# Routing keys of the chosen pairs by comparison of positions with row offsets, instead of one-hots over 50 candidates

## The chip, the cores and the metric

The kernel runs on one core of a Trainium2 chip. The metric is the device time of one execution in microseconds (us). Before the change the median of three runs is 2036.78 us (2036.38 to 2038.27).

## The reference, cut to what matters

The model has two layers. Each is a mixer (five small head groups behind one input projection, then an output projection) followed by PEER, a feed-forward part that picks 16 of 16,384 experts for each of 8 heads and each of 256 tokens. The change lies in the picking:

```python
q  = (xn @ wq).reshape(b, s, 8, 2, 128)
sc = einsum('bshjc,hjkc->bshjk', q, subkeys)         # two score rows of 128 keys per head
top_s, top_i = top_k(sc, 16)                         # 16 best keys of each row
cand = top_s[..., 0, :, None] + top_s[..., 1, None, :]   # 16 x 16 sums
best, ci = top_k(cand, 16)                           # 16 best pairs
i1 = take_along_axis(top_i[..., 0, :], ci // 16)     # first key of each chosen pair
i2 = take_along_axis(top_i[..., 1, :], ci % 16)      # second key
g  = softmax(best)
act = gelu(u_tab[i1*128 + i2] . xn) * g              # then  sum of act * v_tab[i1*128 + i2]
```

Since both rows are sorted, a pair (a, b) can be among the 16 best only if (a+1)(b+1) <= 16. That leaves 50 of 256 sums. The kernel keeps these 50 in 16 rows: row a has `PAIR_LEN[a]` = 16 // (a+1) sums and begins at position `PAIR_OFF[a]`. The chosen positions are numbers from 0 to 49.

## The kernel before

Nothing is gathered. All experts' products are computed densely: 128 blocks of `u_t` and 128 blocks of `v_t` per layer, each a 128x1024 f32 weight tile, are streamed from HBM. The class `Stream` loads a block (`w_raw`, three buffers), rounds it to `w_hi` on ScalarE (line 82) and takes the rest `w_lo = w_raw - w_hi` on VectorE (line 84; 10 of the 612 on GpSimd). `w_hi` and `w_lo` have three buffers each, so a `w_hi` may be written only when TensorE has finished with the block three places earlier. `out_t_job` then does 24 matmuls per block, at lines 235 to 237: `w_hi` with `xh`, `w_hi` with `xl`, `w_lo` with `xh`. `pair_job` runs two blocks and hands the sums to ScalarE (line 930 for `u_t`).

In a PEER phase the blocks are 16 of `wq`, 128 of `u_t`, 128 of `v_t`. The routing runs as background work beside `wq` and the first `u_t` blocks: generators whose steps are emitted between the half pairs (`Background.advance`, with a cost noted at each `yield`). `score_steps(tt)` (lines 787 to 822), for each of two tiles of 128 tokens, has the key scores from TensorE (line 799) and takes the 16 best with five VectorE instructions per row (805 to 809); GpSimd makes the 50 sums `cand` and, in the same way, the 50 sums of keys `ecand` = 128 i1 + i2 (818, 821). `best_steps(tt)` takes the 16 best sums of each head (832 to 836), and then for each head builds a 50x16 one-hot of the chosen positions (846), multiplies it with `ecand` (848) and sums over the 50 (853). Lines 856 to 859 split the result into i1 and i2; three transposes on TensorE and three ScalarE copies (869 to 871) give `i1T`, `i2T`, `gT`.

When both tiles are routed, `gate_step` spreads the gates: 32 groups of 8 tokens per layer, one after each `u_t` pair. `gate_one_hots` builds `a2` (888) and eight `ag` (893) on VectorE, `gate_group` multiplies them on TensorE (903) and applies them (907, 908). The `u_t` results of the first 64 blocks lie in the first half of one large tile `H`; the routing's tables are carved from its second half, so they read as `H` in every row.

The order on each engine is fixed when the program is built: a scheduler simulates the engines and places instructions by readiness and priority, `w_hi` and `w_lo` 300 places ahead. On the chip each engine works its queue in that order.

Of the kernel before, what the change touches and what calls it, by code (L numbers as in the profile page):

```python
# [136 lines left out]
def build(tc, x, mem, w_in, w_kv, w_out, wq, u_t, v_t, subk, pool_w, conv_pw, vec, dist, inv_count, ind, out, depth=2,  # L137
          dbg=None):
    nc = tc.nc
    V, A, G = nc.vector, nc.scalar, nc.gpsimd  # L140
# [14 lines left out]
    with (  # L155
# [17 lines left out]

        ind_t = cp.tile([P, 3, P], F32, name="ind_t")
        ones_m, ind64, ind32 = ind_t[:, 0, :], ind_t[:, 1, :], ind_t[:, 2, :]
        iota_i = cp.tile([P, NPAIR, 16], BF16, name="iota_i")
        G.iota(iota_i, pattern=[[1, NPAIR], [0, 16]], base=0, channel_multiplier=0, allow_small_or_imprecise_dtypes=True)
        iota_f = cp.tile([P, NK], F32, name="iota_f")
        G.iota(iota_f, pattern=[[1, NK]], base=0, channel_multiplier=0, allow_small_or_imprecise_dtypes=True)
        mhalf = cp.tile([P, 1], F32, name="mhalf")  # L180
# [553 lines left out]
        def peer_phase(l, pp, pb):  # L734
            nonlocal vecs

            def psum(shape, name):
                return pb.tile(shape, F32, name=name, tag="misc")

            def acc_tile(i, shape, name):  # L740
                return (pb if i % 2 else accp).tile(shape, F32, name=name, tag="acc")
# [10 lines left out]
            def carve(n, dt=F32):  # L752
                nonlocal o
                s = hf[:, o:o + n]
                o += n
                assert o <= NK * T
                return s if dt is F32 else s.bitcast(dt)

            qT = carve(4096)
            xs = qT[:, 0:2 * D].rearrange("p (a d) -> p a d", a=2)  # L760
            qT = qT.rearrange("p (h j t) -> p h j t", h=8, j=2)
            rms_transposed(pp, psum, xt, xs, vv("norm_ffn"), xh, xl, True)
            sk = carve(2048).rearrange("p (a k) -> p a k", a=16)
            nc.sync.dma_start(sk, subk[l])
# [3 lines left out]
            gT = pt([P, T], "gT")  # L768

            work = [carve(128) for _ in range(2)]  # L770
            oh = [carve(8 * NPAIR, BF16).rearrange("p (n k) -> p n k", k=16) for _ in range(2)]
            pr = [carve(16 * NPAIR).rearrange("p (k n) -> p k n", k=16) for _ in range(2)]
            tabs = []
            for tt in range(2):
                tabs.append(dict(
                    top_s=carve(256).rearrange("p (h j k) -> p h j k", h=8, j=2),
                    top_i=carve(256, U32).rearrange("p (h j k) -> p h j k", h=8, j=2),
                    top_f=carve(256).rearrange("p (h j k) -> p h j k", h=8, j=2),
                    cand=carve(8 * NPAIR).rearrange("p (h n) -> p h n", h=8),
                    ecand=carve(8 * NPAIR).rearrange("p (h n) -> p h n", h=8),  # L780
                    best=carve(P).rearrange("p (h k) -> p h k", h=8),
                    bi=carve(P, U32).rearrange("p (h k) -> p h k", h=8),
                    bib=carve(P // 2, BF16).rearrange("p (h k) -> p h k", h=8),
                    es=carve(P).rearrange("p (h k) -> p h k", h=8),
                    ei=carve(3 * P, I32).rearrange("p (a k) -> p a k", a=3),
                    fin=carve(3 * P).rearrange("p (a k) -> p a k", a=3),
                    gs=carve(8)))
            done = {"q": 0, "routing": False, "u": 0, "g": 0}

            def score_steps(tt):  # L790

                tb = tabs[tt]
                for hq in range(4):
                    while done["q"] < 2 * hq + 2:
                        yield None
                    ps = acc_tile(hq, [P, 4, NK], "ps_sc")
                    for r in range(4):
                        hj = 4 * hq + r
                        nc.tensor.matmul(ps[:, r, :], qT[:, hj // 2, hj % 2, tt * P:(tt + 1) * P], sk[:, hj, :],  # L799
                                         start=True, stop=True)  # L800
# [10 lines left out]
                top_s, top_f = tb["top_s"], tb["top_f"]  # L811
                V.tensor_copy(top_f, tb["top_i"])
                V.tensor_scalar(top_f[:, :, 0, :], top_f[:, :, 0, :], 128.0, None, op0=ALU.mult)
                for dst, src in ((tb["cand"], top_s), (tb["ecand"], top_f)):
                    for a in range(9):
                        n, off = PAIR_LEN[a], PAIR_OFF[a]
                        if a < 8:
                            G.tensor_add(dst[:, :, off:off + n], src[:, :, 1, 0:n],
                                         src[:, :, 0, a:a + 1].to_broadcast([P, 8, n]))
                        else:  # L820
                            G.tensor_add(dst[:, :, off:off + 8], src[:, :, 0, 8:16],
                                         src[:, :, 1, 0:1].to_broadcast([P, 8, 8]))
                yield 0.6

            def best_steps(tt):

                tb = tabs[tt]
                best, bi, cand, ecand = tb["best"], tb["bi"], tb["cand"], tb["ecand"]
                wk = work[tt][:, :NPAIR]
                for h in range(8):  # L830
                    m0, m1 = best[:, h, 0:8], best[:, h, 8:16]
                    V.max(m0, cand[:, h, :])
                    V.max_index(bi[:, h, 0:8], m0, cand[:, h, :])
                    V.match_replace(wk, m0, cand[:, h, :], -3e38)
                    V.max(m1, wk)
                    V.max_index(bi[:, h, 8:16], m1, wk)
                    yield 0.8
                fin, gs = tb["fin"], tb["gs"]
# [3 lines left out]
                V.tensor_copy(tb["bib"], bi)  # L842
                yield 0.6

                def one_hot(h):
                    V.tensor_tensor(out=oh[h % 2], in0=iota_i, in1=tb["bib"][:, h, None, :].to_broadcast([P, NPAIR, 16]),
                                    op=ALU.is_equal)
                    V.tensor_mul(pr[h % 2], oh[h % 2].rearrange("p n k -> p k n"),  # L848
                                 ecand[:, h, None, :].to_broadcast([P, 16, NPAIR]))

                for h in range(8):
                    one_hot(h)
                    V.tensor_reduce(tb["es"][:, h, :], pr[h % 2], axis=AX.X, op=ALU.add)  # L853
                    yield 2.4
                ei = tb["ei"]
                V.tensor_copy(ei[:, 0, :], tb["es"].rearrange("p h k -> p (h k)"))
                V.tensor_scalar(ei[:, 1, :], ei[:, 0, :], 7, None, op0=ALU.arith_shift_right)
                V.tensor_scalar(ei[:, 2, :], ei[:, 0, :], 127, None, op0=ALU.bitwise_and)
                V.tensor_copy(fin[:, 0:2, :], ei[:, 1:3, :])
                yield 1.0  # L860
# [212 lines left out]
```

## Time and profile before

| | us |
|---|---|
| median of three runs | 2036.78 |
| the profiled execution, its own time | 2035.27 |
| its span | 2033.5 |
| TensorE busy | 1973.2 (97%) |
| VectorE busy | 1494.1 (73%) |
| ScalarE busy | 985.4 (48%) |
| GpSimd busy | 165.0 (8%) |

PE is TensorE's matmul side, PEld its weight load, DVE VectorE, ACT ScalarE, POOL GpSimd, SP the engine that issues the DMAs. A line is that of the kernel before. The first layer's PEER phase runs from 173.6 us to about 1020 us; its `u_t` part ends at 669 us. The second layer repeats it some 1006 us later.

### The profile page before, as it was taken

The numbers are of one execution on the slowest core, as the hardware profiler recorded it, in microseconds if no ns is written. First come the engines' busy times: TensorE is split into PE (matmuls) and PEld (weight loads), VectorE is DVE, ScalarE is ACT, GpSimd is POOL, SyncE is SP. The second block draws the span as 40 slices with busy tenths as digits, with TensorE's granted clock in tenths as the row PEclk, the third lists the DMA queues.
The fourth block names the chain that finished last, engine by engine and source line by source line (L and its number), as shares of the span: only waits on it lengthen the run. The fifth ranks groups of instructions, "written<-read, shape, count | busy, mean of one in ns | idle before, by whom it ended". The sixth has DMA issues, their size and how long they took to land.

```text
span 2033.5 us, 33742 instructions
## 1 busy us (share of the span) xinstructions
PE 1973.2 (97%) x13122; PEld 1811.5 (89%) x13122; DVE 1494.1 (73%) x2809; ACT 985.4 (48%) x1474; POOL 165.0 (8%) x201
## 2 busy tenths in 40 slices
PE   8889999999999999999999999999999999999999
PEld 7878999899999888888898789999999998888887
DVE  6975899878898655555578669997789975555555
ACT  6664445344444544444466644444444344444443
POOL 3720101000000000000036201010000000000000
PEclk9999999999999999999999999999999999999999
DMA  5325445444444555555543254445434445555554
GB/s 212 115 74 175 167 150 172 162 153 143 144 137 156 199 195 189 194 189 194 189 169 111 86 169 166 162 151 172 149 136 146 140 152 194 188 193 190 194 189 156
DMA packets 92768, 331.50 MB, mean 163 GB/s; under 512 B 10816, under 2 KB 11712, under 8 KB 92352
## 3 DMA queue, kind: packets, MB, share of 16 engines
q1 hardware_dynamic: 92608, 329.34, 46.7%
q8 instruction: 103, 1.69, 0.3%
q14 instruction: 57, 0.47, 0.1%
HBM read 328.25 MB, written 1.05 MB: 162 GB/s over the span
## 4 chain that ended last, share of the span: by engine, by line
PE 82%; DVE 10%; ACT 3%; issue 3%; POOL 3%; DMA 1%; SPq 0%; DVEq 0%; POOLq 0%; ACTq 0%
PE ps_mm L237 13%; PE ps_mm L235 13%; PE ps_mm L236 13%; PE acc_v L265 11%; PE acc_v L268 11%; PE acc_v L264 11%; PE ps_g L903 5%; DVE w_lo L84 3%; DVE H L848 2%; POOL cv_ac L433 1%; ACT w_hi L82 1%; DVE ag L893 1%; DVE H L853 1%; PE ps_sc L799 1%; PE acc_o L264 1%
## 5 line engine op out<-in xcount | busy, mean ns | idle before, releaser
L84 DVE TENSOR_TENSOR w_lo<-w_raw,w_hi 128x1024 fp32r<-128x1024 f32 x602 | 743.0, 1235 | 394.6 <-ACT w_hi L82 392.6
L82 ACT CAST w_hi<-w_raw 128x1024 fp32r<-128x1024 f32 x612 | 641.5, 1049 | 786.7 <-PE ps_mm L236 443.0
L237 PE MATMUL ps_mm<-xh,w_lo 128*128 128x256 f32 x2624 | 748.3, 286 | 16.8 <-DVE w_lo L84 16.5
L235 PE MATMUL ps_mm<-xh,w_hi 128*128 128x256 f32 x2624 | 752.2, 288 | 2.6 <-ACT H L930 2.3
L236 PE MATMUL ps_mm<-xl,w_hi 128*128 128x256 f32 x2624 | 746.2, 285 | 0.1
L237 PEld LDWEIGHTS ps_mm<-xh,w_lo 128*128 128x128 f32 x2624 | 504.7, 192 | 22.9 <-DVE w_lo L84 21.9
L235 PEld LDWEIGHTS ps_mm<-xh,w_hi 128*128 128x128 f32 x2624 | 504.0, 192 | 4.7 <-ACT H L930 3.3
L236 PEld LDWEIGHTS ps_mm<-xl,w_hi 128*128 128x128 f32 x2624 | 505.4, 193 | 1.0 <-DVE xl L226 0.6
L265 PE MATMUL acc_v<-w_lo,a_hi 128*128 128x512 f32 x1016 | 316.5, 392 | 0.0
L268 PE MATMUL acc_v<-w_hi,a_lo 128*128 128x512 f32 x1016 | 315.4, 392 | 0.0
L264 PE MATMUL acc_v<-w_hi,a_hi 128*128 128x512 f32 x1016 | 274.1, 391 | 0.0
L268 PEld LDWEIGHTS acc_v<-w_hi,a_lo 128*128 128x128 f32 x1016 | 191.0, 188 | 42.3
L264 PEld LDWEIGHTS acc_v<-w_hi,a_hi 128*128 128x128 f32 x1016 | 190.9, 188 | 41.7
L265 PEld LDWEIGHTS acc_v<-w_lo,a_hi 128*128 128x128 f32 x1016 | 191.0, 188 | 40.6
L941 ACT CAST a_hi<-H 128x512 fp32r<-128x512 f32 x128 | 79.3, 621 | 154.1 <-PE acc_v L265 150.2
L943 DVE TENSOR_TENSOR a_lo<-H,a_hi 128x512 fp32r<-128x512 f32 x128 | 88.5, 693 | 77.5 <-ACT a_hi L941 77.5
L893 DVE TENSOR_SCALAR ag<-iota_f,i1T,gT 128x128 f32<-128x128 f32 x512 | 142.0, 343 | 0.0
L903 PE MATMUL ps_g<-ag,a 128*128 128x128 f32 x1024 | 125.8, 275 | 1.1 <-DVE ag L893 1.1
L903 PEld LDWEIGHTS ps_g<-ag,a 128*128 128x128 f32 x1024 | 120.6, 192 | 1.5 <-DVE ag L893 1.5
L888 DVE TENSOR_TENSOR a<-iota_f,i2T 128x1024 f32<-128x1024 f32 x64 | 77.8, 1218 | 0.0
L908 DVE TENSOR_TENSOR H<-ps_g,H 128x240 f32<-128x240 f32 (+31 forms) x128 | 66.2, 523 | 0.1
L195 POOL MEMSET mm_kz<- 128x1024 f32 x2 | 1.9, 951 | 698.1 <-DMA w_raw<-w_kv 698.1
(242 smaller groups left out, 1464.2 us busy)
## 6 DMA issues: line engine op xcount, KB each, us to landing
w_raw<-u_t SPq DMA_DIRECT2D x256, 512.0 KB, 3.3
w_raw<-v_t SPq DMA_DIRECT2D x256, 512.0 KB, 3.2
w_raw<-w_in SPq DMA_DIRECT2D x40, 512.0 KB, 3.3
w_raw<-wq SPq DMA_DIRECT2D x32, 512.0 KB, 3.4
w_raw<-w_out SPq DMA_DIRECT2D x20, 512.0 KB, 3.2
w_raw<-w_kv SPq DMA_DIRECT2D x8, 512.0 KB, 3.4
H<-subk SPq DMA_DIRECT2D x2, 1024.0 KB, 4.8
mem_t<-mem SPq DMA_DIRECT2D x4, 256.0 KB, 6.3
```

Of the source, the lines that this page charges most:

```text
L82: self.nc.scalar.copy(hi, r)
L84: (self.nc.gpsimd if on_pool else self.nc.vector).tensor_sub(lo, r, hi.bitcast(F32))
L235: nc.tensor.matmul(ps, wh, xh[:, c, :], start=(c == 0), stop=False)
L236: nc.tensor.matmul(ps, wh, xl[:, c, :], start=False, stop=False)
L237: nc.tensor.matmul(ps, wl, xh[:, c, :], start=False, stop=(c == NC - 1))
L264: nc.tensor.matmul(accs[tt][hf], ah[:, s], hi[:, n], start=start, stop=False)
L265: nc.tensor.matmul(accs[tt][hf], ah[:, s], lo[:, n], start=False, stop=False)
L268: nc.tensor.matmul(accs[tt][hf], al[:, s], hi[:, n], start=False, stop=False)
L893: V.tensor_scalar(ag[:, t, :], iota_f, i1T[:, k:k + 1], gT[:, k:k + 1], op0=ALU.is_equal, op1=ALU.mult)
L903: nc.tensor.matmul(ps[:, t, :], a2[:, 4 * q + t, :], ag[:, 4 * q + t, :], start=True, stop=True)
L941: A.copy(ah, src)
L943: V.tensor_sub(al, src, ah.bitcast(F32))
```

## The change

The first key of a chosen pair at position n is the sum, over the 16 rows a, of [n >= `PAIR_OFF[a]`] times (key of row a minus key of row a-1). The same comparisons with the row lengths give the start of n's row; n minus that start is the place b in the row, and the second key is the sum over k of [b >= k] times (key k minus key k-1). All heads of a tile are done in one instruction each, on 128x(8x16x16) bf16 operands, with the sum over 16 as four halvings (1024, 512, 256, 128 elements). The key differences `diff` are made at the end of `score_steps` (817 to 821 in the new file) and ScalarE spreads them to `dx` (854). `ecand` and its GpSimd sums go, as do the conversions at 856 to 859. The large bf16 tiles lie where the queries `qT` were.

```diff
-        iota_i = cp.tile([P, NPAIR, 16], BF16, name="iota_i")
+        iota_b = cp.tile([P, 16, 16], BF16, name="iota_b")
+        offs = cp.tile([P, 16, 16], BF16, name="offs")
+        steps = cp.tile([P, 16, 16], BF16, name="steps")
+        for a in range(16):
+            G.memset(offs[:, a, :], float(PAIR_OFF[a]))
+            G.memset(steps[:, a, :], float(PAIR_LEN[a - 1] if a else 0))
...
-            oh = [carve(8 * NPAIR, BF16).rearrange("p (n k) -> p n k", k=16) for _ in range(2)]
-            pr = [carve(16 * NPAIR).rearrange("p (k n) -> p k n", k=16) for _ in range(2)]
+            qb = q_flat.bitcast(BF16).rearrange("p (n a k) -> p n a k", n=32, a=16)
+            ge, dx, prod = qb[:, 0:8], (qb[:, 8:16], qb[:, 16:24]), qb[:, 24:32]
+            tree = [carve(n, BF16).rearrange("p (m k) -> p m k", k=16) for n in (512, 256, 128)]
...
-                V.tensor_scalar(top_f[:, :, 0, :], top_f[:, :, 0, :], 128.0, None, op0=ALU.mult)
-                for dst, src in ((tb["cand"], top_s), (tb["ecand"], top_f)):
+                V.tensor_copy(diff[:, :, :, 0:1], tf[:, :, :, 0:1])
+                for j in range(2):
+                    V.tensor_sub(diff[:, j, :, 1:], tf[:, j, :, 1:], tf[:, j, :, :15])
...
+            def pick(dst, x, marks_, deltas):
+                if x is not None:
+                    V.tensor_tensor(out=ge, in0=x[:, :, None, :].to_broadcast([P, 8, 16, 16]),
+                                    in1=marks_[:, None, :, :].to_broadcast([P, 8, 16, 16]), op=ALU.is_ge)
+                    yield 1.2
+                V.tensor_mul(prod, ge, deltas)
+                yield 1.2
+                src = prod.rearrange("p h a k -> p (h a) k")
+                for n, t in enumerate(tree + [dst]):
+                    pair = src.rearrange("p (m two) k -> p m two k", two=2)
+                    V.tensor_add(t, pair[:, :, 0, :], pair[:, :, 1, :])
+                    src = t
+                yield 1.3
...
+                for j in range(2):
+                    A.copy(dx[j], tb["diff"][:, j, :, :, None].to_broadcast([P, 8, 16, 16]))
...
-                for h in range(8):
-                    one_hot(h)
-                    V.tensor_reduce(tb["es"][:, h, :], pr[h % 2], axis=AX.X, op=ALU.add)
-                    yield 2.4
+                yield from pick(k1, bib, offs, dx[0])
+                yield from pick(bb, None, None, steps[:, None, :, :].to_broadcast([P, 8, 16, 16]))
+                V.tensor_sub(bb, bib, bb)
+                yield from pick(k2, bb, iota_b, dx[1])
```

The scheduler makes a new order from this. VectorE, first layer, in the middle of the first tile's picking, before:

```order
L84 TENSOR_TENSOR w_lo<-w_raw,w_hi 128x1024
L806 MAX_INDEX H<-H,ps_sc 128x8
L862 RECIPROCAL H<-H 128x8
L853 TENSOR_REDUCE H<-H 128x16
L846 TENSOR_TENSOR H<-iota_i,H 128x800
L853 TENSOR_REDUCE H<-H 128x16
L846 TENSOR_TENSOR H<-iota_i,H 128x800
L809 MAX_INDEX H<-H 128x8
L806 MAX_INDEX H<-H,ps_sc 128x8
L84 TENSOR_TENSOR w_lo<-w_raw,w_hi 128x1024
L863 TENSOR_TENSOR H<-H 128x128
L848 TENSOR_TENSOR H<-H 128x800
```

The same place after (839 is the product, 844 the halvings; 811 to 814 are the second tile's best keys):

```order
L84 TENSOR_TENSOR w_lo<-w_raw,w_hi 128x1024
L812 MATCH_REPLACE H<-H,ps_sc 128x128
L810 MAX H<-ps_sc 128x8
L876 TENSOR_TENSOR H<-H 128x128
L810 MAX H<-ps_sc 128x8
L839 TENSOR_TENSOR H<-H 128x2048
L84 TENSOR_TENSOR w_lo<-w_raw,w_hi 128x1024
L813 MAX H<-H 128x8
L811 MAX_INDEX H<-H,ps_sc 128x8 x2
L844 TENSOR_TENSOR H<-H 128x1024
L814 MAX_INDEX H<-H 128x8
L84 TENSOR_TENSOR w_lo<-w_raw,w_hi 128x1024
```

There is one large picking instruction between two `w_lo` where there were several. VectorE where the first gate one-hots are made, while the second tile is still being routed, before (`a` is `a2`, numbered by buffer):

```order
L853 TENSOR_REDUCE H<-H 128x16
L846 TENSOR_TENSOR H<-iota_i,H 128x800
L888 TENSOR_TENSOR a_4624<-iota_f,i2T 128x1024
L888 TENSOR_TENSOR a_4635<-iota_f,i2T 128x1024
L893 TENSOR_SCALAR ag<-iota_f,i1T,gT 128x128 x7
L853 TENSOR_REDUCE H<-H 128x16
L84 TENSOR_TENSOR w_lo<-w_raw,w_hi 128x1024
L846 TENSOR_TENSOR H<-iota_i,H 128x800
L893 TENSOR_SCALAR ag<-iota_f,i1T,gT 128x128
L84 TENSOR_TENSOR w_lo<-w_raw,w_hi 128x1024
```

And after (901 and 906 are the old 888 and 893; 859 and 860 take the second tile's best sums):

```order
L84 TENSOR_TENSOR w_lo<-w_raw,w_hi 128x1024
L859 MATCH_REPLACE H<-H 128x50
L901 TENSOR_TENSOR a_4194<-iota_f,i2T 128x1024
L901 TENSOR_TENSOR a_4205<-iota_f,i2T 128x1024
L906 TENSOR_SCALAR ag<-iota_f,i1T,gT 128x128 x11
L84 TENSOR_TENSOR w_lo<-w_raw,w_hi 128x1024
L860 MAX H<-H 128x8
L906 TENSOR_SCALAR ag<-iota_f,i1T,gT 128x128 x2
L84 TENSOR_TENSOR w_lo<-w_raw,w_hi 128x1024
```

The bunch of gate one-hots between two `w_lo` stays, with eleven `ag` instead of seven, and no picking beside it. On ScalarE the spreading copies stand among the `w_hi`; the second tile's, after:

```order
L82 CAST w_hi<-w_raw 128x1024
L854 COPY H<-H 128x2048 x2
L82 CAST w_hi<-w_raw 128x1024
L943 ACTIVATE H<-ps_mm 128x512
L82 CAST w_hi<-w_raw 128x1024
L882 COPY i1T<-ps_rt 128x128
```

Before, nothing stood there but `w_hi` and the line 930 activations. The DMA order is unchanged. The 32 gate groups of a layer begin 7 `u_t` pairs earlier.

## Rows read from the trace of the kernel before

**Rows 1.** The page, busy time of each engine.
```profile
PE 1973.2 (97%) x13122; PEld 1811.5 (89%) x13122; DVE 1494.1 (73%) x2809; ACT 985.4 (48%) x1474; POOL 165.0 (8%) x201
```
**Rows 2.** Windows: stretch, length, busy and count by engine, PEclk, DMA share, GB/s.
```profile
230.00:270.00 40.00, 40.00 (x338) 40.00 (x337) 39.90 (x199) 19.06 (x22) 6.37 (x18) 1.00 0.48 163
270.00:392.00 122.00, 113.90 (x911) 111.19 (x911) 118.80 (x245) 51.55 (x62) 6.38 (x18) 0.99 0.46 156
392.00:416.00 24.00, 24.00 (x203) 24.00 (x202) 10.86 (x11) 11.34 (x18) 0.00 (x0) 1.00 0.55 198
1276.00:1396.00 120.00, 110.07 (x886) 106.75 (x885) 117.40 (x242) 50.30 (x60) 6.37 (x18) 1.00 0.44 150
```
**Rows 3.** PE timeline around 649 us: start, us, instruction.
```profile
648.79 0.28 PE L235 MATMUL ps_mm<-xh,w_hi 128*128 128x256 f32 x1
648.91 0.28 PE L236 MATMUL ps_mm<-xl,w_hi 128*128 128x256 f32 x1
```
**Rows 4.** Waits from 265 to 395 us: us in total, times, longest.
```profile
ACT w_hi L82 <- DMA w_raw<-u_t: 35.5, 12, 6.4
...
PE ps_mm L237 <- DVE w_lo L84: 5.8, 6, 1.5
```
**Rows 5.** The chain of waits, 346 to 358 us: start, us, what.
```profile
346.38 1.20 DVE w_lo L84
347.58 1.66 DVE H L848
...
351.95 1.21 DVE a L888 x2
...
354.15 1.19 DVE ag L893 x5
```
**Rows 6.** Windows: 372 to 375.2 us, columns as in rows 2.
```profile
372.00:375.20 3.20, 3.20 (x17) 3.20 (x16) 3.20 (x5) 0.37 (x1) 0.00 (x0) 0.50 0.73 247
```
**Rows 7.** DVE timeline from 349 to 359 us.
```profile
349.37 1.21 DVE L84 TENSOR_TENSOR w_lo<-w_raw,w_hi 128x1024 fp32r<-128x1024 f32 x1
350.50 0.97 DVE L853 TENSOR_REDUCE H<-H 128x16 f32<-128x800 f32 x1
...
351.88 2.34 DVE L888 TENSOR_TENSOR a<-iota_f,i2T 128x1024 f32<-128x1024 f32 x2
354.15 1.86 DVE L893 TENSOR_SCALAR ag<-iota_f,i1T,gT 128x128 f32<-128x128 f32 x7
...
356.84 1.20 DVE L84 TENSOR_TENSOR w_lo<-w_raw,w_hi 128x1024 fp32r<-128x1024 f32 x1
```
**Rows 8.** DVE by line and form, 230 to 392 us: count, busy us, mean ns.
```profile
L84 DVE TENSOR_TENSOR w_lo<-w_raw,w_hi 128x1024 fp32r<-128x1024 f32 x49 | 59.1, 1210 | 4.5 <-ACT w_hi L82 4.5
L848 DVE TENSOR_TENSOR H<-H 128x800 f32<-128x800 bf16 x16 | 27.1, 1698 | 0.0
L853 DVE TENSOR_REDUCE H<-H 128x16 f32<-128x800 f32 x16 | 15.4, 970 | 0.0
L846 DVE TENSOR_TENSOR H<-iota_i,H 128x800 bf16<-128x800 bf16 x16 | 8.9, 562 | 0.0
...
L863 DVE TENSOR_TENSOR H<-H 128x128 f32<-128x128 f32 x2 | 0.6, 285 | 0.0
...
L859 DVE CAST H<-H 128x256 f32<-128x256 int32 x1 | 0.3, 272 | 0.0
```
**Rows 9.** ACT by line and form, whole span.
```profile
L82 ACT CAST w_hi<-w_raw 128x1024 fp32r<-128x1024 f32 x612 | 641.5, 1049 | 786.7 <-PE ps_mm L236 443.0 <-PE acc_v L268 205.4 <-DMA w_raw<-u_t 74.1
...
L370 ACT ACTIVATE mem_t<-mem_t 128x2048 f32<-128x2048 f32 x1 | 1.9, 1911 | 0.3 <-DVE ml L299 0.3
```
**Rows 10.** ACT timeline at 414 us; in brackets the idle before, and its releaser.
```profile
414.07 1.05 ACT L82 CAST w_hi<-w_raw 128x1024 fp32r<-128x1024 f32 x1 [1.83 <-PE ps_mm L236]
```
**Rows 11.** POOL timeline from the start.
```profile
0.34 0.10 POOL L1066 MEMSET const-uint8-127<- 128x1 uint8 x1
...
16.97 0.67 POOL L214 TENSOR_TENSOR rn_rs<-rn_ms,mhalf 128x1 f32<-128x1 f32 x1 [14.51 <-DVE rn_ms L212]
```

More of the change, by code (lines that the diff above doesn't have):

```diff
@@ L175, in build @@
         ones_m, ind64, ind32 = ind_t[:, 0, :], ind_t[:, 1, :], ind_t[:, 2, :]
-        iota_i = cp.tile([P, NPAIR, 16], BF16, name="iota_i")
-        G.iota(iota_i, pattern=[[1, NPAIR], [0, 16]], base=0, channel_multiplier=0, allow_small_or_imprecise_dtypes=True)
+        iota_b = cp.tile([P, 16, 16], BF16, name="iota_b")
+        G.iota(iota_b, pattern=[[1, 16], [0, 16]], base=0, channel_multiplier=0, allow_small_or_imprecise_dtypes=True)
+        offs = cp.tile([P, 16, 16], BF16, name="offs")
[3 more added lines that the diff above has]
+            G.memset(steps[:, a, :], float(PAIR_LEN[a - 1] if a else 0))
         iota_f = cp.tile([P, NK], F32, name="iota_f")
@@ L757, in carve @@
                 return s if dt is F32 else s.bitcast(dt)
-            qT = carve(4096)
-            xs = qT[:, 0:2 * D].rearrange("p (a d) -> p a d", a=2)
-            qT = qT.rearrange("p (h j t) -> p h j t", h=8, j=2)
+            q_flat = carve(4096)
+            xs = q_flat[:, 0:2 * D].rearrange("p (a d) -> p a d", a=2)
+            qT = q_flat.rearrange("p (h j t) -> p h j t", h=8, j=2)
             rms_transposed(pp, psum, xt, xs, vv("norm_ffn"), xh, xl, True)
@@ L779, in peer_phase @@
                     cand=carve(8 * NPAIR).rearrange("p (h n) -> p h n", h=8),
-                    ecand=carve(8 * NPAIR).rearrange("p (h n) -> p h n", h=8),
+                    diff=carve(P, BF16).rearrange("p (j h k) -> p j h k", j=2, h=8),
                     best=carve(P).rearrange("p (h k) -> p h k", h=8),
@@ L783, in peer_phase @@
                     bib=carve(P // 2, BF16).rearrange("p (h k) -> p h k", h=8),
-                    es=carve(P).rearrange("p (h k) -> p h k", h=8),
-                    ei=carve(3 * P, I32).rearrange("p (a k) -> p a k", a=3),
+                    bb=carve(P // 2, BF16).rearrange("p (h k) -> p h k", h=8),
                     fin=carve(3 * P).rearrange("p (a k) -> p a k", a=3),
@@ L810, in score_steps @@
                         yield 1.2
-                top_s, top_f = tb["top_s"], tb["top_f"]
+                top_s, top_f, cand, diff = tb["top_s"], tb["top_f"], tb["cand"], tb["diff"]
                 V.tensor_copy(top_f, tb["top_i"])
-                V.tensor_scalar(top_f[:, :, 0, :], top_f[:, :, 0, :], 128.0, None, op0=ALU.mult)
-                for dst, src in ((tb["cand"], top_s), (tb["ecand"], top_f)):
[L815 to L822, printed above, removed]
@@ L823, in score_steps @@
-                yield 0.6
+                tf = top_f.rearrange("p h j k -> p j h k")
+                V.tensor_copy(diff[:, :, :, 0:1], tf[:, :, :, 0:1])
+                for j in range(2):
+                    V.tensor_sub(diff[:, j, :, 1:], tf[:, j, :, 1:], tf[:, j, :, :15])
+                for a in range(9):
+                    n, off = PAIR_LEN[a], PAIR_OFF[a]
+                    if a < 8:
+                        G.tensor_add(cand[:, :, off:off + n], top_s[:, :, 1, 0:n],
+                                     top_s[:, :, 0, a:a + 1].to_broadcast([P, 8, n]))
+                    else:
+                        G.tensor_add(cand[:, :, off:off + 8], top_s[:, :, 0, 8:16],
+                                     top_s[:, :, 1, 0:1].to_broadcast([P, 8, 8]))
@@ new lines, in score_steps @@
+                yield 1.0
+            def pick(dst, x, marks_, deltas):
[11 more added lines that the diff above has]
+                yield 1.3
@@ L825, in best_steps @@
             def best_steps(tt):
                 tb = tabs[tt]
-                best, bi, cand, ecand = tb["best"], tb["bi"], tb["cand"], tb["ecand"]
+                best, bi, cand = tb["best"], tb["bi"], tb["cand"]
                 wk = work[tt][:, :NPAIR]
+                for j in range(2):
+                    A.copy(dx[j], tb["diff"][:, j, :, :, None].to_broadcast([P, 8, 16, 16]))
                 for h in range(8):
@@ L837, in best_steps @@
                     yield 0.8
-                fin, gs = tb["fin"], tb["gs"]
+                fin, gs, bib, bb = tb["fin"], tb["gs"], tb["bib"], tb["bb"]
                 gx = fin[:, 2, :].rearrange("p (h k) -> p h k", h=8)
@@ L841, in best_steps @@
                 A.activation(gx, gx, AF.Exp)
[L842 to L849, printed above, removed]
-                for h in range(8):
-                    one_hot(h)
-                    V.tensor_reduce(tb["es"][:, h, :], pr[h % 2], axis=AX.X, op=ALU.add)
-                    yield 2.4
[L855 to L860, printed above, removed]
+                V.tensor_copy(bib, bi)
+                yield 0.5
+                k1, k2 = [fin[:, j, :].rearrange("p (h k) -> p h k", h=8) for j in range(2)]
+                yield from pick(k1, bib, offs, dx[0])
+                yield from pick(bb, None, None, steps[:, None, :, :].to_broadcast([P, 8, 16, 16]))
+                V.tensor_sub(bb, bib, bb)
+                yield from pick(k2, bb, iota_b, dx[1])
                 V.tensor_reduce(gs, gx, axis=AX.X, op=ALU.add)
```

## The prediction

> **What bounds the kernel now.** I read the page first: TensorE is busy 97% of the span, VectorE 73% [rows 1]. So TensorE's work is the floor, and a change on VectorE can only win back time in which TensorE waits for it. The windows say where. From 270 to 392 us VectorE is busy 118.8 of 122 us, and TensorE gets only 911 matmuls through; right after, from 392 to 416 us, it does 203 in 24 us, 0.118 us each, with VectorE half idle [rows 2]. From start to start two matmuls of a block are 0.12 us apart [rows 3]; the 0.28 us in those rows is a modelled end, so TensorE's busy time hides most of a stall and the count must be used instead. Of 911 matmuls at 0.118 to 0.120 us, 107.7 to 109.3 us are work and 12.7 to 14.3 us are stall. In the second layer, 1276 to 1396 us, 886 matmuls make 104.7 to 106.3 of 120 us: 13.7 to 15.3 us of stall [rows 2]. Together 26.4 to 29.6 us; I use 28.
>
> The waits name the cause: matmuls of line 237 wait for `w_lo`, and ScalarE's `w_hi` waits for late DMAs, whose buffers come free only when VectorE has made an earlier `w_lo` [rows 4]. The chain of waits there runs on VectorE through `w_lo`, 848, and the gate one-hots 888 and 893 [rows 5]. [...]
>
> How much other work does VectorE have room for? A block is 24 matmuls, 2.88 us. `w_lo` takes 1.13 us from its start to the next instruction's [rows 7], so 1.75 us per block are left. There is a cushion: `w_hi` may start when TensorE has finished the block three before, so `w_lo` can be ready 2 x 2.88 - 1.05 - 1.21 = 3.5 us early [rows 8, 9].
>
> **The change part by part.** *Removed, per layer, on VectorE.* The mean durations in the routing stretch are 562, 1698 and 970 ns for lines 846, 848 and 853, 3.23 us per head [rows 8]. The layer has 16 such sets (8 heads, 2 tiles; the 16 in these rows are all of one layer's): 51.7 us. The four instructions at 856 to 859 and the scaling at 813 are ten, at most 0.27 us each [rows 8]; I take 2.3 us. Sum 54.0 us.
>
> *Added.* Line 84 with 1024 f32 elements takes 1.210 us and line 863 with 128 takes 0.285 [rows 8]: 1.03 ns per element and 0.15 fixed. Line 846, all bf16, takes 0.562 for 800: (0.562 - 0.15) / 800 = 0.51 ns per element, half. No row shows the new shapes. From below I know of nothing faster than line 846; from above there are two rows: line 84 (one element per 1.03 ns) and line 848 ((1.698 - 0.15) / 800 = 1.93 ns), whose bf16 operand is read across, 16 elements apart. The new comparisons and products are bf16 throughout and every operand runs along 16 neighbours, as in 846, so I take that price: 1.20 us for 2048 elements, 0.68, 0.42 and 0.28 for 1024, 512 and 256, and 0.285 for the last halving, which mostly writes f32. Per tile: two comparisons and three products, 5 x 1.20 = 6.0; three sums of 16, 3 x 1.66 = 5.0; the subtraction 0.3; the differences (one copy, two subtractions of 120 elements, at most 0.285 each) 0.7. That is 12.0 us per tile and 24.0 per layer. At line 84's price the same list is 5 x 2.26 + 3 x 2.6 + 1.0 = 20.1 per tile, 40.2 per layer; at line 848's, 5 x 4.1 + 3 x 4.3 + 1.0 = 34.4 per tile, 68.8 per layer.
>
> [...]
>
> *Sum on VectorE.* From 230 to 392 us it is busy 39.9 + 118.8 = 158.7 us, and TensorE's 338 + 911 matmuls need 147 to 150 [rows 2]. With 54.0 out and 24.0 in it has 128.7: about 87% of what TensorE needs, instead of 107%. On average the stall has no ground any more.
>
> *What stays.* In places the queue is still dense. The gate one-hots made ahead, two `a2` and now eleven `ag`, stand between two `w_lo`: 2.27 us for the pair of `a2` and 1.86 / 7 = 0.27 us per `ag` [rows 7], with the small instruction ahead of them about 5.4 us, against 1.75 and a cushion of 3.5 that the second tile's first best-sum instructions, all together between two `w_lo`, have partly spent. Before, 6.3 us stood at the same place (350.50 to 356.84). I take 1.5 us per layer. And ScalarE gets four spreading copies per layer. The nearest row, 2048 f32 elements, is 1.91 us [rows 9]; from below it could be half (16-bit data), from above twice (one element read 16 times). A single copy is hidden: ScalarE sits idle for 1.83 us ahead of each second `w_hi`, waiting for TensorE [rows 10]. The second tile's two stand together, 3.8 us, push the next `w_hi` back by 2 us, and use up cushion just before the one-hots: 0.5 us per layer. In sum 2 us per layer stay, 4 in all.
>
> *New waits.* The large tiles lie where the queries were, so a first-tile copy must wait until TensorE has read those heads' queries for the second tile's scores; behind it in ScalarE's queue stands the next `w_hi`, and behind that `w_lo` and the matmuls. In the new order these score matmuls stand at the start of a block two before the one whose `w_hi` the copy follows, and that `w_hi` itself needs the block three before it done; so I take nothing, and from above one block, 2.88 us per layer, which is inside the range. The second tile's copies also wait for `diff`, which VectorE makes in the stretch just ahead; behind them stands the `w_hi` already counted.
>
> *Hidden.* 32 small fills on GpSimd at the start, about 0.1 us each, lie in its 14.5 us of idle time before 16.97 us [rows 11]; without that cover they would cost 3 us. `ecand` frees GpSimd, which nobody waits for. The gates begin 7 pairs earlier; a gate's matmuls cost the same wherever they stand, since beside them TensorE has no gap. DMAs are neither added nor moved.
>
> **The sum.** 28 - 4 = 24 us from the profiled execution's 2035.27 us gives 2011.3. The median of the three runs lies 1.5 us above that execution, so I predict 2012.8 us.
>
> **Rivals.**
> 1. *Half speed.* The new operations go at one element per cycle, as line 84. For: six operands are broadcasts, and no row shows one of 2048. Against: 846 has one too. Then VectorE's load falls by 54.0 - 40.2 = 13.8 us per layer, to 145 of the 147 to 150 that TensorE needs; a queue with no slack keeps about half of the stall. Gain 13 us: 2024.
> 2. *Bunching.* The stall is made by places, not by the average: one-hots and copies keep 6 us per layer instead of 2. For: the chain shows 888 and 893 beside 848 [rows 5]. Gain 16: 2021.
> 3. *ScalarE takes `w_lo`'s place.* Each of the eight copies delays a `w_hi` by its full 1.91 us: 15 of the 24 come back, gain 9: 2028. Against: ScalarE is busy only 51.6 of 122 us there [rows 2].
> 4. *Slower.* The broadcast and halved operands are read at line 848's rate. The place is the same 34 comparisons, products and halvings per layer. VectorE's load rises by 68.8 - 54.0 = 14.8 us per layer in a stretch where it is already full, and all of it is stall: 2 x 14.8 = 30 us, 2067. It turns at 54 us added per layer, 1.5 ns per element. Against: no operand is read across.
> 5. *No change.* The stall is not VectorE's but that of the late DMAs [rows 4], which wait for other things. Against: where VectorE is half idle, `w_hi` waits only for TensorE [rows 10]. 2037.
>
> **How the numbers follow.** Forecast 0.66, with a range of its own from 2007 (all 29.6 us gone) to 2018; bunching 0.12, half speed 0.07, ScalarE 0.04, no change 0.05, slower 0.06. The range that leaves out no more than 2 in 10 reaches from 2007 to 2025, past bunching and half speed. About 0.2%, 4 us, is what a measurement of this kernel can tell from no change. Faster: 0.66 + 0.12 + 0.07 + 0.04 = 0.89; within 4 us 0.05; slower 0.06.
>
> **What the profile after would show.** The comparisons and products at 1.2 us (2.3 means rival 1, 4 rival 4). From 270 us on, a count of matmuls near 0.12 us each, VectorE with idle time in which it waits for `w_hi`, and no lower clock. If `w_hi` waits behind the 2048-element copies, rival 3; if `w_lo` is late only behind 901 and 906, rival 2. The prediction is wrong if VectorE is well below full there and TensorE still loses more than 5 us per layer.

## The result, and the profile after

The changed kernel takes 2008.95 us in the median of four runs (2008.58 to 2009.85), the kernel before 2037.44 in the same rounds: a ratio of 0.9861, 95% interval 0.9844 to 0.9878, or 28.5 us. The forecast was 2012.8 us, range 2007 to 2025. The profiled execution takes 2009.29 us, 26.0 us less than the profiled one of before; its span is 2007.1. Single executions of the kernel before lie between 2035.2 and 2038.9 us, so the medians tell the gain better.

On the page, TensorE's busy share goes from 97% [rows 1] to 98%, VectorE's from 73 to 72%. VectorE's busy time falls by 54.0 us, 27.0 per layer where the prediction had 54.0 - 24.0 = 30.0. For TensorE the counts tell more, as before:

```profile
PE 1965.0 (98%) x13122; PEld 1808.6 (90%) x13122; DVE 1440.1 (72%) x2791; ACT 1005.3 (50%) x1482; POOL 153.0 (8%) x197
```

The windows of [rows 2], and three shorter ones (length, busy and count of PE, PEld, DVE, ACT and POOL, PEclk, DMA share, GB/s):

```profile
230.00:270.00 40.00, 40.00 (x338) 40.00 (x337) 38.71 (x192) 22.83 (x24) 3.05 (x9) 1.00 0.47 166
270.00:392.00 122.00, 122.00 (x1026) 122.00 (x1026) 106.81 (x272) 63.02 (x85) 3.17 (x9) 1.00 0.50 171
1276.00:1396.00 120.00, 120.00 (x1011) 120.00 (x1010) 103.48 (x265) 60.84 (x85) 3.17 (x9) 1.00 0.50 170
...
266.00:298.00 32.00, 32.00 (x270) 32.00 (x269) 31.30 (x87) 16.72 (x20) 0.25 (x1) 1.00 0.51 176
...
340.00:364.00 24.00, 24.00 (x202) 24.00 (x202) 20.01 (x29) 13.10 (x16) 0.00 (x0) 1.00 0.51 185
```

From 270 to 392 us TensorE does 1026 matmuls where it did 911, one per 0.119 us; in the second layer 1011 for 886. At 0.119 us each that is 13.7 and 14.9 us. No wait of TensorE is left from 230 to 392 us, the granted clock stays at 1.00, and the waits of `w_hi` for late DMAs, 35.5 us [rows 4], are gone although no DMA was moved: they were a consequence. Look at the short windows too: from 266 to 298 us, the first tile's picking, VectorE is still busy 31.3 of 32 us.

The new operations and `w_lo`, by line and form from 230 to 392 us (count, busy us, mean ns, idle before), answering to [rows 8]:

```profile
L84 DVE TENSOR_TENSOR w_lo<-w_raw,w_hi 128x1024 fp32r<-128x1024 f32 x52 | 63.4, 1220 | 15.1 <-ACT w_hi L82 15.0
L839 DVE TENSOR_TENSOR H<-H 128x2048 bf16<-128x2048 bf16 x4 | 4.9, 1217 | 0.0
L844 DVE TENSOR_TENSOR H<-H 128x1024 bf16<-128x1024 bf16 x6 | 4.1, 684 | 0.0
L844 DVE TENSOR_TENSOR H<-H 128x512 bf16<-128x512 bf16 x6 | 2.5, 423 | 0.0
...
L836 DVE TENSOR_TENSOR H<-H,offs 128x2048 bf16<-128x2048 bf16 x2 | 2.4, 1217 | 0.0
...
L844 DVE TENSOR_TENSOR H<-H 128x256 bf16<-128x256 bf16 x6 | 1.7, 283 | 0.1
```

They were priced at 1.20, 0.68, 0.42 and 0.28 us. And `w_lo` now waits for `w_hi`, 15 us in all: VectorE has idle time.

### The profile page after: what moved, and what is told of

It reads as the page before. It is cut to its first block, busy times and chain, and to the rows that moved or that the text cites. A ratio compares the mean times of both kernels' runs of the same rounds, so it can differ in the third digit from the quotient of the medians.

```text
span 2007.1 us, 33754 instructions
## 1 busy us (share of the span) xinstructions
PE 1965.0 (98%) x13122; PEld 1808.6 (90%) x13122; DVE 1440.1 (72%) x2791; ACT 1005.3 (50%) x1482; POOL 153.0 (8%) x197
## 4 chain that ended last, share of the span: by engine, by line
PE 89%; DVE 4%; POOL 2%; ACT 2%; issue 1%; DMA 0%; SPq 0%; DVEq 0%; POOLq 0%; ACTq 0%
PE ps_mm L240 15%; PE ps_mm L241 15%; PE ps_mm L242 15%; PE acc_v L270 12%; PE acc_v L273 12%; PE acc_v L269 12%; PE ps_g L916 6%; POOL cv_ac L438 1%; DVE w_lo L84 1%; PE ps_sc L804 1%; ACT w_hi L82 1%; PE acc_o L269 1%; PE acc_o L273 1%; PE acc_o L270 1%; PE ps_t L227 0%
## 5 line engine op out<-in xcount | busy, mean ns | idle before, releaser
L921 DVE TENSOR_TENSOR H<-ps_g,H 128x184 f32<-128x184 f32 (+31 forms) x128 | 58.8, 463 | 1.2 <-ACT H L920 1.2
```

## The experiments

Each run is compared with the kernel before in its own rounds (medians 2036.6 to 2037.6 us). "Added" is VectorE's work per layer against the changed kernel: half the difference of VectorE's busy time on the pages, 1440.1 us for the changed kernel (for the last two runs against the kernel before, 1494.1). It comes out lower than a sum of the durations of the instructions, as in the expectations, because one overlaps the next (1.22 us long, 1.13 from its start to the next start). "Place" is that of the second tile's transposes in TensorE's queue, in matmuls from the first of the layer's PEER phase; in the kernel before it is 1884. The wait is that of these transposes (line 880 in the changed kernel) in the first layer; in the second it is the same.

| run | added, us | place | wait, us | median, us | ratio to before, 95% |
|---|---|---|---|---|---|
| changed kernel | 0 | 1566 | 0 | 2008.95 | 0.9844 to 0.9878 |
| big operations twice | 11.2 | 1692 | 2.8 | 2020.14 | 0.9903 to 0.9936 |
| pick in f32 | 15.9 | 1692 | 7.7 | 2033.96 | 0.9976 to 0.9995 |
| all operations twice | 19.5 | 1692 | 11.0 | 2038.02 | 0.9996 to 1.0015 |
| product read across | 22.8 | 1692 | 6.2 | 2037.03 | 0.9987 to 1.0006 |
| all twice, larger yields | 18.6 | 1836 | 2.5 | 2019.38 | 0.9895 to 0.9928 |
| smaller yields | 0.7 | 1500 | 3.3 | 2021.12 | 0.9906 to 0.9939 |
| copies three times | 0.2 | 1524 | 0 | 2018.72 | 0.9893 to 0.9926 |
| gates late | -0.5 | 1566 | 0 | 2007.52 | 0.9834 to 0.9866 |
| `ecand` kept | 0.2 | 1566 | 0 | 2008.62 | 0.9836 to 0.9869 |
| before, half the heads | -23.0 | 1446 | 0 | 2007.27 | 0.9833 to 0.9865 |
| before, 6 of 8 heads | -11.8 | 1884 | 0 | 2020.72 | 0.9905 to 0.9938 |

### More work for VectorE

*Comparisons and products twice.*

```diff
-                    V.tensor_tensor(out=ge, in0=x[:, :, None, :].to_broadcast([P, 8, 16, 16]),
+                    for _ in range(2): V.tensor_tensor(out=ge, in0=x[:, :, None, :].to_broadcast([P, 8, 16, 16]),
...
-                V.tensor_mul(prod, ge, deltas)
+                for _ in range(2): V.tensor_mul(prod, ge, deltas)
```

> The changed kernel with every comparison and every product of the picks issued twice: 10 more operations of 1.22 us per layer, 12.2 us on VectorE, nothing else. Theory A (average load: VectorE has 128.7 of the 147 to 150 us that TensorE needs from 230 to 392 us, so 18 to 21 us per layer are free): no change, 2009 us (2007 to 2011). Theory L (local load: in the changed kernel VectorE is busy 125.5 of 134 us from 230 to 364 us, 8.5 us are free, and the cushion of 3.5 us can be spent once; 12 us per layer are free in all, not spread evenly): 0 to 4 us per layer come back, 2009 to 2017 us. Rival B (the gain does not come from VectorE's load but from the gates' earlier place, or from the work taken off GpSimd): no change, 2009 us.

*All of the pick twice*, the halvings too.

```diff
-                    V.tensor_add(t, pair[:, :, 0, :], pair[:, :, 1, :])
+                    for _ in range(2): V.tensor_add(t, pair[:, :, 0, :], pair[:, :, 1, :])
```

> The changed kernel with every comparison, product and halving of the picks issued twice: 12.2 us for the comparisons and products and 6 x 1.6 = 9.7 us for the halvings, 21.9 us more on VectorE per layer. Theory A (18 to 21 us per layer are free): 1 to 4 us per layer come back, 2011 to 2017 us. Theory L (12 us per layer are free): 10 us per layer come back, 2029 us. Rival B (VectorE's load is not the cause): 2009 us.

2020.1 and 2038.0 us: the numbers of A and of rival B, near no change, are refuted, and L, the nearest, is too low both times. 19.5 us per layer, less than the 27.0 that the change saves, give the whole gain back. But the loss was at a place that neither A nor L had named. The waits of TensorE from 230 to 400 us, all operations twice:

```profile
PE ps_rt L880 <- DVE H L844: 11.0, 1, 11.0
PE ps_g L916 <- DVE H L921: 0.7, 1, 0.7
```

No `w_lo` is late. There is one wait of 11.0 us: the transposes that turn the second tile's keys stand at a fixed place in TensorE's queue, and the last halving has not been done. The place is fixed when the program is built; here it is 126 matmuls, 15.0 us, behind that of the changed kernel. VectorE and then TensorE there (start, us, what; in brackets the idle time before, and its releaser):

```profile
379.25 1.22 DVE L84 TENSOR_TENSOR w_lo<-w_raw,w_hi 128x1024 fp32r<-128x1024 f32 x1 [0.60 <-ACT w_hi L82]
...
380.65 2.48 DVE L836 TENSOR_TENSOR H<-H,iota_b 128x2048 bf16<-128x2048 bf16 x2
383.17 2.48 DVE L839 TENSOR_TENSOR H<-H 128x2048 bf16<-128x2048 bf16 x2
385.69 3.64 DVE L844 TENSOR_TENSOR H<-H 128x1024 bf16<-128x1024 bf16 x8
```

```profile
389.38 0.69 PE L880 MATMUL ps_rt<-ident,H 128*128 128x128 f32 x2 [11.01 <-DVE H L844]
390.81 6.67 PE L916 MATMUL ps_g<-ag,a 128*128 128x128 f32 x32 [0.75 <-DVE H L921]
397.25 0.36 PE L240 MATMUL ps_mm<-xh,w_hi 128*128 128x256 f32 x1
```

and the windows of that stretch:

```profile
376.00:380.00 4.00, 2.37 (x20) 2.13 (x19) 3.29 (x8) 1.39 (x2) 0.00 (x0) 1.00 0.64 201
380.00:384.00 4.00, 0.00 (x0) 0.00 (x0) 3.90 (x5) 0.00 (x0) 0.00 (x0) 0.89 0.50 175
384.00:388.00 4.00, 0.00 (x0) 0.00 (x0) 3.83 (x6) 0.00 (x0) 0.00 (x0) 0.50 0.00 0
...
392.00:396.00 4.00, 4.00 (x21) 4.00 (x20) 1.92 (x4) 1.77 (x6) 0.00 (x0) 0.50 0.00 0
396.00:400.00 4.00, 4.00 (x33) 4.00 (x33) 4.00 (x14) 0.84 (x2) 0.00 (x0) 0.90 0.00 0
```

TensorE stands still while VectorE works off its rest: the whole last pick, twelve operations, stands in VectorE's queue behind the last `w_lo`, with no other `w_lo` in between. In the changed kernel three of them stand between the six operations of the same pick, from 352.6 to 361.0 us. Then TensorE runs at a granted clock of 0.50: from 392 to 396 us it does 21 matmuls, and 33 in the next 4 us at 0.90. That is the price per layer: 11.7 us of waiting and about 2.6 at the lower granted clock (the gate's 32 matmuls take 6.4 us, where 3.8 would do at 0.119 us each), 14.3 of the measured 29.1 / 2 = 14.5.

*The pick in f32.*

```diff
-            qb = q_flat.bitcast(BF16).rearrange("p (n a k) -> p n a k", n=32, a=16)
-            ge, dx, prod = qb[:, 0:8], (qb[:, 8:16], qb[:, 16:24]), qb[:, 24:32]
-            tree = [carve(n, BF16).rearrange("p (m k) -> p m k", k=16) for n in (512, 256, 128)]
+            qb, qc = [t.rearrange("p (n a k) -> p n a k", n=16, a=16) for t in (q_flat, carve(4096))]
+            ge, dx, prod = qb[:, 0:8], (qb[:, 8:16], qc[:, 0:8]), qc[:, 8:16]
+            tree = [t.rearrange("p (m k) -> p m k", k=16) for t in (carve(1024), qc[:, 8:10].rearrange("p n a k -> p (n a k)"), carve(256))]
```

> The changed kernel with the pick's tiles (comparison result, deltas, products, halvings) in f32 instead of bf16; positions, offsets and steps stay bf16. If only all-16-bit operations run at 0.51 ns per element, each 2048-element operation takes 2.26 us as line 84's price says, the halvings 1.21, 0.68 and 0.42, and 16 us per layer are added. Theory A: no change, 2009 us. Theory L: 16 - 12 = 4 us per layer come back, 2017 us. Rival 1 of the prediction as it was priced there: 2024 us. If f32 costs nothing (the operations stay at 1.22 us), 2009 us, and bf16 is not needed.

2034.0 us, later than every theory said. The forms (columns as above):

```profile
L839 DVE TENSOR_TENSOR H<-H 128x2048 f32<-128x2048 f32 x4 | 9.1, 2286 | 0.0
L844 DVE TENSOR_TENSOR H<-H 128x1024 f32<-128x1024 f32 x6 | 7.3, 1218 | 0.0
...
L836 DVE TENSOR_TENSOR H<-H,offs 128x2048 f32<-128x2048 bf16 x2 | 4.6, 2282 | 0.0
```

The price per operation was as expected (2.286 us for 2.26), so bf16 is what makes the pick cheap: without it 3 of the 28.5 us are left. The comparison reads bf16 only and is slow for its f32 result alone: 2.282 us for 1.217.

*One more product, read across.*

```diff
+                V.tensor_mul(prod, ge.rearrange("p h a k -> p h k a"), deltas)
                 V.tensor_mul(prod, ge, deltas)
```

> The changed kernel with one more product ahead of each of the picks' products, all bf16, whose first operand is read across, 16 elements apart; its result is overwritten. Six more operations of 2048 elements per layer. At the price of line 848 of the kernel before (1.93 ns per element) one takes 4.1 us and the six 24.6 us per layer; at one element per cycle 2.26 and 13.6 us; at the rate of its neighbours 1.22 and 7.3 us. At 4.1 us: theory A gives 4 to 7 us per layer, 2017 to 2023 us; theory L 12.6 us per layer, 2034 us; rival B no change. At 2.26 us: A 2009, L 2012. At 1.22 us: 2009 by all.

Its form, then the two longest of TensorE's waits:

```profile
L838 DVE TENSOR_TENSOR H<-H 128x2048 bf16<-128x2048 bf16 x4 | 16.2, 4058 | 0.0
```

```profile
PE ps_rt L880 <- DVE H L844: 6.2, 1, 6.2
PE ps_mm L242 <- DVE w_lo L84: 1.9, 2, 0.9
...
```

4.06 us, the price of line 848, though all three operands are bf16: reading across is what costs there; the same product read along takes 1.207 us in this run. The time is 2037.0, near L's 2034. Here `w_lo` is late too, as in the kernel before. At one of the two places 4.7 us of other work stand between two `w_lo` (283.6 to 288.3 us), 4.0 of them this product; that is longer than the cushion of 3.5 us that the prediction estimated from [rows 8, 9].

*What the four runs have in common.* In all of them the transposes stand at place 1692. In the three in which no `w_lo` is late, the added work less the wait is nearly the same: 11.2 - 2.8 = 8.4, 15.9 - 7.7 = 8.2, 19.5 - 11.0 = 8.5 us per layer. So much is free ahead of that date; it is not the room of the changed kernel, whose date comes 15.0 us sooner. An estimate from the traces leads from one to the other: in these 15.0 us VectorE has seven more `w_lo` to make, 7.9 us at 1.13 us each, and with the 2.6 us that the changed kernel has to spare (below) 9.7 us are free at the later place.

### The same work at another place

*All twice, with larger yields*, and *the changed kernel with smaller yields*.

In the first, on top of the doubled operations:

```diff
-                yield 1.2
+                yield 1.8
...
-                yield 1.3
+                yield 1.9
```

and in the second, alone:

```diff
-                yield 1.2
+                yield 0.6
...
-                yield 1.3
+                yield 0.65
```

> The run with every operation of the picks issued twice (21.9 us more on VectorE per layer; 2038 us, with one wait of 11.0 us of TensorE's transposes for the last halving of the second tile) with larger yields in the picks (1.8 and 1.9 for 1.2 and 1.3), so that the routing is spread over more pairs: in TensorE's queue the second tile's transposes now stand 144 matmuls, 6 blocks or 17.3 us, later; VectorE's work is the same. Theory D (what is too much for VectorE ends in a wait of these transposes, which stand at a fixed place of TensorE's queue: a date that the work misses or not): the wait of 11.0 us goes, 2009 to 2012 us. Theories A and L (VectorE's load decides): 2030 to 2038 us.

> The changed kernel with half the yields in the picks (0.6 and 0.65 for 1.2 and 1.3), nothing else: the same instructions, but in TensorE's queue the second tile's transposes stand 66 matmuls, 2.75 blocks or 7.9 us, earlier; in the changed kernel they come 2.4 us after the last halving has ended. Theory D: the transposes wait 7.9 - 2.4 = 5.5 us per layer, less what VectorE gains from its 4 us of idle time in that stretch, 1.5 to 5.5 us per layer, 2012 to 2020 us. Theories A and L (load alone, which is the same): 2009 us.

The waits of TensorE in the two, in this order:

```profile
PE ps_rt L880 <- DVE H L844: 2.5, 1, 2.5
PE ps_g L916 <- DVE H L921: 0.8, 1, 0.8
```

```profile
PE ps_rt L880 <- DVE H L844: 3.3, 1, 3.3
PE ps_g L916 <- DVE H L921: 0.8, 1, 0.8
```

This shows theory D's mechanism from both sides. With the transposes 6 blocks later nearly the same added work costs 10 us instead of 29; with them 2.75 blocks earlier a kernel with no more operations than the changed one loses 12.2 us: per layer 3.3 + 0.8 us of waiting, and of the other 2.0 us about 1.3 at the granted clock of 0.67 behind it (last section). The yields also set how closely the picks stand together on VectorE, and the two runs do not separate that from the date; but no `w_lo` is late in either, and the waits shown are all that TensorE has from 230 to 420 us. D's number for the larger yields, 2009 to 2012, was too low. It took the 17.3 us that the transposes come later as won, but VectorE has six more `w_lo` to make in them, 6.8 us; 2.5 us of the wait stay, and from 392 to 416 us, where it falls, the granted clock was 0.86 in the mean.

### ScalarE, gates, GpSimd

*Each spreading copy three times.*

```diff
-                    A.copy(dx[j], tb["diff"][:, j, :, :, None].to_broadcast([P, 8, 16, 16]))
+                    for _ in range(3): A.copy(dx[j], tb["diff"][:, j, :, :, None].to_broadcast([P, 8, 16, 16]))
```

> The changed kernel with each spreading copy on ScalarE issued three times. The first tile's copies then stand three in a row, 5.7 us: the next w_hi has 1.83 us of idle time ahead of it and the cushion of 3.5 us, so at most 0.4 us each comes through. The second tile's stand six in a row, 11.4 us: 11.4 - 1.8 - 3.5 = 6 us per layer come back. Theory (ScalarE has slack and a cushion, but a bunch of copies that outlasts them delays w_hi and so w_lo and TensorE): 2020 to 2023 us. Rival (ScalarE's copies are hidden whatever their number, since it is busy only 63 of 122 us): 2009 us. Rival 3 of the prediction (every copy delays by its full time): eight more copies per layer, 15 us each layer, 2039 us.

2018.7 us, a little below the expected 2020 to 2023; TensorE's waits from 230 to 400 us:

```profile
PE ps_mm L240 <- ACT H L943: 2.2, 2, 1.8
PE ps_mm L242 <- DVE w_lo L84: 0.5, 1, 0.5
```

A bunch of copies does come through, by 4.9 us per layer for the expected 6, but by these waits mostly over another way: behind the copies in ScalarE's queue stand the activations (943) that empty TensorE's results.

*The gates 7 pairs later*, and *GpSimd's additions put back*.

```diff
-                if not done["routing"] or done["g"] == T:
+                if not done["routing"] or done["g"] == T or done.update(late=done.get("late", 0) + 1) or done["late"] <= 7:
```

```diff
-                for a in range(9):
+                for a, d, s in [(a, d, s) for d, s in ((cand, top_s), (tb["ecand"], top_f)) for a in range(9)]:
```

> The changed kernel with the gates held back by 7 pairs, to about the place that they have in the kernel before (their first one-hots are still made early). Theory (a gate's matmuls cost TensorE the same wherever they stand, and the gain is VectorE's load in the routing stretch): no change, 2009 us, within 4. Rival B (part of the gain is the earlier start of the gates, which leaves fewer of them after the last pair): 2013 us or more.

> The changed kernel with GpSimd's 18 additions per layer for the candidates' keys put back; nobody reads their result. Theory (nobody waits for GpSimd): no change, 2009 us, within 2. Rival (GpSimd's work slows VectorE beside it, or delays the candidates' scores that VectorE needs next): 2011 us or more, with VectorE operations longer than 1.22 us beside it or a wait for cand.

2007.5 and 2008.6 us: neither can be told from the changed kernel. The gates' place and GpSimd have no part in the gain that these runs could show.

### The kernel before with less work

```diff
-                    one_hot(h)
-                    V.tensor_reduce(tb["es"][:, h, :], pr[h % 2], axis=AX.X, op=ALU.add)
+                    if h % 2 == 0:
+                        one_hot(h)
+                        V.tensor_reduce(tb["es"][:, h, :], pr[0], axis=AX.X, op=ALU.add)
+                    else:
+                        V.tensor_copy(tb["es"][:, h, :], tb["es"][:, h - 1, :])
```

In the second run the condition is `h % 4 < 3`.

> The kernel before with the one-hot, the product and the sum made for every second head only; the other heads get a copy of their neighbour's result, so half of the keys are not computed. VectorE loses 8 sets of 3.23 us per layer and gets 8 copies of about 0.2 us: 24 us less per layer, where the whole change took 30 away; GpSimd's additions, ScalarE's queue and the form of the operations stay as before. Theory (VectorE's load alone): nearly the whole gain, 2009 to 2014 us. Rival 5 (the late DMAs have another cause): no change, 2037 us. Rival B (the gates' place, GpSimd): no more than half of the gain, 2023 us or more.

> The kernel before with the one-hot, the product and the sum for 6 of 8 heads; two heads get a copy of their neighbour's result, so a quarter of the keys is not computed. 4 sets of 3.23 us per layer go and 4 copies of 0.2 come: 12 us less per layer, where the stall is 13 to 15 us per layer. If the stall is one for one what VectorE has too much of: 1 to 3 us per layer stay, 2010 to 2014 us. If it is made by each set where it stands (bunching, rival 2 of the prediction): a quarter of the gain, 2030 us.

Half the heads: 2007.3 us, the whole gain with nothing of the change but 23.0 us less for VectorE per layer, and the order that the scheduler made of it; the gates begin one pair earlier than in the kernel before, not seven. That refutes rival 5 and, with the gates held back and `ecand` kept above, rival B. Six of eight heads: 2020.7, between the two expectations. The windows of the latter, then the first of them with half the heads:

```profile
266.00:298.00 32.00, 30.75 (x251) 29.95 (x250) 32.00 (x71) 15.84 (x18) 0.00 (x0) 1.00 0.45 151
298.00:340.00 42.00, 42.00 (x351) 41.87 (x350) 40.91 (x129) 22.76 (x29) 7.34 (x18) 1.00 0.56 176
340.00:364.00 24.00, 22.09 (x180) 21.50 (x180) 24.00 (x43) 7.00 (x9) 0.00 (x0) 1.00 0.40 137
364.00:392.00 28.00, 27.40 (x228) 27.20 (x227) 19.38 (x27) 12.38 (x15) 0.00 (x0) 1.00 0.61 202
```

```profile
266.00:298.00 32.00, 32.00 (x270) 32.00 (x269) 32.00 (x87) 17.51 (x20) 0.00 (x0) 1.00 0.50 166
```

11.8 us less bought 8 us per layer. With six of eight heads most of what stays is where VectorE is busy 100%, at 266 to 298 and 340 to 364 us (251 and 180 matmuls for 270 and 202), while it is idle for 8.6 of 28 us right behind. So the mean does not set the stall. But a full stretch alone does not tell it either: with half the heads VectorE is busy in all of the same 32 us, and TensorE does its 270 matmuls. A queue that is just in time and one that is late look the same in the busy share.

## Why the prediction was right, and where it was not

**Cause.** Right. VectorE's queue made the stall, the late DMAs and the granted clock of 0.50 [rows 6] followed from it; half the heads left out, where the granted clock is 1.00 in every window from 230 to 392 us, shows this without any other part of the change. The estimate of the stall, 28 us for two layers, stands against 28.6 by the matmul counts and 28.5 by the medians (26.0 by the two profiled executions).

**Prices.** Right: 1.217 us for 1.20, and the copies 1.894 for the 1.91 of [rows 9]. The broadcast operands read at line 846's rate, (1.217 - 0.15) / 2048 = 0.52 ns per element by the prediction's estimate of 0.15 us fixed, for 0.51, so rival 1 (half speed) and rival 4 (read across) did not come. Both prices are real: 2.286 us in the f32 run and 4.058 us for the product read across. What the prediction and an expectation call one element per cycle is line 84's measured 1.03 ns per element; no trace here shows a cycle.

**What stays.** This term was mis-sized: 4 us predicted, no wait of TensorE measured. The forecast lies 3.9 us above the median, and this term makes that up. The bunch of gate one-hots, on VectorE, is as long as was worked out (columns: start, us, what):

```profile
312.04 2.35 DVE L901 TENSOR_TENSOR a<-iota_f,i2T 128x1024 f32<-128x1024 f32 x2
314.31 2.90 DVE L906 TENSOR_SCALAR ag<-iota_f,i1T,gT 128x128 f32<-128x128 f32 x11
317.13 1.22 DVE L84 TENSOR_TENSOR w_lo<-w_raw,w_hi 128x1024 fp32r<-128x1024 f32 x1
```

But ahead of the matmuls that need this `w_lo` TensorE now has the first gate's to do:

```profile
317.70 2.62 PE L916 MATMUL ps_g<-ag,a 128*128 128x128 f32 x22
...
320.39 0.28 PE L242 MATMUL ps_mm<-xh,w_lo 128*128 128x256 f32 x1
```

That `w_lo` is done at 318.35, and by the order of the buffers it belongs to the block whose first matmul with `w_lo` is the one at 320.39: 2.0 us to spare. Without the gate's 2.4 us it would have been late by less than a microsecond. Here the prediction counted the one-hots and left out the matmuls that they feed. The second tile's pair of copies was also to cost 0.5 us:

```profile
303.88 3.69 ACT L854 COPY H<-H 128x2048 bf16<-128x2048 bf16 x2
307.48 1.04 ACT L82 CAST w_hi<-w_raw 128x1024 fp32r<-128x1024 f32 x1
```

They push `w_hi` to 307.48, and no wait of TensorE follows. Three times as many do cost something, though by the named waits mostly through the activations behind them and not, as rival 3 had it, through `w_hi`. What the prediction put at nothing did cost nothing: no new wait of TensorE shows, the fills at the start do not delay the first PEER phase (173.25 us for 173.62), and the gates' place and GpSimd's additions are the two runs above.

**The sum on VectorE.** As an average it came out nearly right; as a room for more work it failed, though that did not show in the time. "About 87% of what TensorE needs" set 128.7 us against 147 to 150. Measured, VectorE is busy 38.7 + 106.8 = 145.5 us, 90% of the 162 that TensorE's 338 + 1026 matmuls fill, since a TensorE that no longer waits asks for more in the same window: 52 `w_lo` for 49, and gates. The 16.5 us of idle time (18 to 21 by the prediction) are not even, 0.7 us from 266 to 298 and 4 from 340 to 364, and the picks cannot use what comes after their date: 11.2 us of added work per layer already cost 5.6 us of time per layer. So rival 1 was priced far too low at 2024: the f32 run gave 2034. Rival 2's idea, that places count and not the mean, holds, but for the picking and its date, not for the one-hots that it named.

**The date.** No step of the prediction asked when the second tile's keys are needed. In the changed kernel the last halving and the transposes stand like this, on VectorE and on TensorE:

```profile
360.74 0.28 DVE L844 TENSOR_TENSOR H<-H 128x128 f32<-128x128 bf16 x1
```

```profile
363.58 0.38 PE L880 MATMUL ps_rt<-ident,H 128*128 128x128 f32 x2
```

2.6 us were to spare. The change brings these transposes forward in TensorE's queue by 318 matmuls, 13 blocks; another 2.75 blocks, as the smaller yields show, and 12 us of the gain would have gone. That the change made its date, by a margin that the prediction never looked at, was luck. In the kernel before that date was far off; its last operation on the keys and its transposes, on VectorE and on TensorE:

```profile
392.01 0.28 DVE L859 CAST H<-H 128x256 f32<-128x256 int32 x1
```

```profile
413.99 0.49 PE L867 MATMUL ps_rt<-ident,H 128*128 128x128 f32 x3
```

The keys were ready 21.7 us ahead.

What is not settled is why the scheduler built the orders so: in the kernel before late transposes and picking between the `w_lo`, where the excess makes `w_lo` late; in most of the loaded runs a `w_lo` that is never late, and the excess in one wait at the transposes. The product read across, which has both, points to the length of single instructions between two `w_lo`; this was not separated from the order.

## What to carry to other kernels

Relief for an engine that feeds the bound is worth the stall and no more: here 23 us per layer taken from VectorE gave the same as 27, and 12 gave 16 of 28 us. Neither the mean busy share nor that of the fullest stretch tells how much is enough; the count of matmuls in short stretches shows where the bound engine loses. After a stall is gone the feeding engine's other work in the same window rises (52 `w_lo` for 49 here); count the room in the pace of the engine that no longer waits. And look up the next date by which the moved work must be done (here transposes in an in-order queue), since a miss cost the wait here, 11.0 us in one run, and then about 2.6 us at a lower granted clock. That place moved from build to build here, so read it anew in each.

## What was not expected of the hardware

The wait of TensorE in the run with all operations twice, 11.0 us and 0.7 behind it, costs almost 3 us per layer more than itself: the granted clock fell to 0.50 while TensorE stood, from 378 to 389 us, and was still 0.50 from 392 to 396, with TensorE at work again. After the wait of 3.3 us in the changed kernel with smaller yields it was 0.67 from 360 to 364:

```profile
356.00:360.00 4.00, 0.72 (x7) 0.51 (x6) 3.82 (x6) 1.04 (x1) 0.00 (x0) 1.00 0.42 139
360.00:364.00 4.00, 3.15 (x15) 2.92 (x16) 1.53 (x7) 3.53 (x12) 0.00 (x0) 0.67 0.35 129
```

There 15 matmuls were done in 3.15 us of work, where 26 fit at 0.119 us: about 1.3 us lost. Before the change the same was to be seen: in the first layer's stall at 368 to 372 us TensorE did 18 matmuls, and in the 3.2 us behind it 17 at a granted clock of 0.50 [rows 6].

And a product that is bf16 in all operands took 4.06 instead of 1.22 us when one operand was read 16 elements apart.
